# A down-projection in seven products of half operands instead of eight

## The chip, the cores and the metric

The kernel runs on one core of one Trainium2 chip. The metric is the device time of one execution in microseconds, lower is better. Matmuls run on TensorE (PE, with its weight loads as PEld), elementwise work on VectorE (DVE) and ScalarE (ACT), small work and some transfers on GpSimd (POOL), and most transfers are issued by SyncE (SP).

## What is computed

One block of a streaming encoder over 512 tokens of width 1024: a state-space mixer and a latent attention side by side, a cross-attention to 256 memory tokens, and a feed-forward part with a causal convolution, each added to the residual x. The feed-forward part and the end are what matters here:

```python
u = causal_depthwise_conv(h @ w_up, conv_w, conv_b)      # h: 512 x 1024, w_up: 1024 x 5632
g, val = jnp.split(u, 2, axis=-1)
x = x + (jax.nn.silu(g) * val) @ w_down                  # 512 x 2816 times 2816 x 1024
return rmsnorm(x, norm_final_w)
```

## The kernel before, in words

All operands are float32. Before a matmul each is split into a high and a low part of the type that TensorE takes (`split`, L92: a cast on ScalarE, then a subtraction on VectorE), and `mm3` (L101 to L105) makes three matmuls of each product: high by high, high by low, low by high. So one k-tile of 128 for one token tile of 128 is three matmuls of 512 columns.

Weights come in pages. `wload` (L145) has SP load 512 KB into one of three raw buffers (`wr`), `wsplit` (L150) splits it into one of four pairs (`wh`, `wl`), and `wpage` (L162) does both.

The up-projection runs over 11 pairs j of feature tiles (L1139). A pass makes two tiles of the gate half and two of the value half: 24 matmuls each into one of three accumulator banks, a convolution of three taps (`conv`, L1125: one ScalarE and two VectorE operations), the gate (`gate`, L1133), and in `evac` (L1151) the product of the two, 128 features by 512 tokens, which is split into high and low there and then (`acts`, L1112 to L1117, 22 tiles). `h3t` (L1054) holds the split input of the up-projection in the tiles tagged Ah and Al, `cbuf` the convolution's buffers.

The down-projection is `down` (L1163): the tokens are four tiles of 128, the output is two halves of 512 columns (`nh`), k runs over 22 tiles, two to a page. `down(0, ...)` makes the left half for all four token tiles, so its 11 pages serve 24 matmuls each; `down(1, (0, 1))` and `down(1, (2, 3))` make the right half for two token tiles at a time and load and split the 11 pages again. In the last call the last token tile is worked in two halves of 256 columns, and the last three pages are held back and run bank by bank, so that the sums of one bank run beside the matmuls of the next. Each finished bank is added to x in SBUF (L1193) and squared and summed (`sq_part`, L196). `finish` (L1198) adds the sums, raises them to -0.5 on POOL, scales one half on VectorE and one on ScalarE by that factor and the norm's weights (`frow`), and stores them from SP's and ScalarE's queues.

The order of instructions on each engine and queue is set when the program is built: a scheduler places them by program order among those that are ready in its own timing. The banks of PSUM are acc (3), tr (2), s (2) and pv (1). Buffers with one tag are handed on when the last reader of the earlier tile is done.

Of the kernel before, what the change touches and what calls it, by code (L numbers as in the profile page):

```python
# [62 lines left out]
def tile_block(ctx, tc, x, mem, positions, norm_mix_w, w_in, ssd_conv_w, ssd_conv_b, ssd_dt_bias,  # L63
# [37 lines left out]
    def mm3(acc, lhs, rhs, first, last):  # L101
        (lh, ll), (rh, rl) = lhs, rhs
        nc.tensor.matmul(acc, lhsT=lh, rhs=rh, start=first, stop=False)  # L103
        nc.tensor.matmul(acc, lhsT=lh, rhs=rl, start=False, stop=False)  # L104
        nc.tensor.matmul(acc, lhsT=ll, rhs=rh, start=False, stop=last)  # L105
# [1006 lines left out]
    acts = []  # L1112
    for tag in ("Bh", "Bl"):
        tl = base.tile([P, 4, 2, T], F32R, name="actB", tag=tag, bufs=1)
        acts += [tl[:, i] for i in range(4)]
    acts += [page("act") for _ in range(5)]
    acts += [k4([P, 2, T], "act", F32R) for _ in range(9)]  # L1117
# [21 lines left out]
    for j in range(FM // 2):  # L1139
# [8 lines left out]
        for m in range(2):  # L1148
            mi = 2 * j + m

            def evac(a):  # L1151
                th = ths[m]
                nc.vector.tensor_tensor(th, th, conv(a, FM + mi, "uv"), ALU.mult)
                split(acts[mi][:, 0], acts[mi][:, 1], th)
            gemm_fm(pv_, m, h3t, T, evac)

# [4 lines left out]
    nc.vector.memset(ssf, EPS)  # L1161

    def down(nh, ts_, staggered=False):  # L1163
        full, halves = (slice(0, 512),), (slice(0, 256), slice(256, 512))
        cols = {t: halves if staggered and t == ts_[-1] else full for t in ts_}
        accs = {}
        for t in ts_:
            for c in cols[t]:
                accs[t, c.start] = (acc_bank() if len(accs) < 3 else s_bank())[:, 0:c.stop - c.start]
        held = []  # L1170

        def add(t, kp, page, c):
            hi, lo = page
            for k in range(2):
                kt = 2 * kp + k
                mm3(accs[t, c.start], (acts[kt][:, 0, tsl(t)], acts[kt][:, 1, tsl(t)]), (hi[:, k, c], lo[:, k, c]),
                    kt == 0, kt == FM - 1)

        for kp in range(FM // 2):
            v = w_ffn_down[0][kp * 2 * P:(kp + 1) * 2 * P, nh * 512:(nh + 1) * 512].rearrange("(k p) c -> p k c", p=P)  # L1180
            page = wpage(v, 2, 512)
            if staggered and kp >= FM // 2 - 3:
                held.append((kp, page))
            else:
                for t in ts_:
                    for c in cols[t]:
                        add(t, kp, page, c)
        for t in ts_:
            for i, c in enumerate(cols[t]):
                for kp, page in held:  # L1190
                    add(t, kp, page, c)
                xs_ = xt[t][:, nh * 512 + c.start:nh * 512 + c.stop]
                nc.vector.tensor_tensor(xs_, accs[t, c.start], xs_, ALU.add)  # L1193
                sq_part(xs_, ssf[:, t, 1 + nh + i:2 + nh + i], fin[:, 2, c], float(D) ** -0.5)
            if nh:
                finish(t, 2 + len(cols[t]))

    def finish(t, n):  # L1198
        rs = small([P, 1], "rs")
        nc.gpsimd.tensor_tensor(rs, ss_total(ssf[:, t, 0:n]), neg_half, ALU.pow)  # L1200
        a, b = xt[t][:, 0:512], xt[t][:, 512:]
        nc.vector.scalar_tensor_tensor(b, b, rs, frow[:, 512:], ALU.mult, ALU.mult)
        nc.sync.dma_start(out[0, tsl(t), 512:], b)
        nc.scalar.activation(a, a, AF.Copy, scale=rs)
        nc.scalar.dma_start(out[0, tsl(t), 0:512], a)

    down(0, range(NT))
    for t in range(NT):
        nc.vector.tensor_tensor(xt[t][:, 0:512], xt[t][:, 0:512], frow[:, 0:512], ALU.mult)
# [27 lines left out]
```

## Time and profile before

| what | us |
|---|---|
| median of 3 runs (lowest, highest) | 984.88 (982.55, 985.73) |
| the profiled execution, its own time | 982.37 |
| its span, first to last instruction | 980.6 |
| TensorE busy, granted clock | 966.8, 0.999 |
| VectorE busy | 667.3 |
| ScalarE busy | 522.2 |
| POOL busy | 187.3 |

The span is what the trace covers; the profiled execution's own time has 1.8 us around it. Busy times are shares of the span and stages differ, so the stretch of the down-projection, from about 853 us on, is read by itself below. A matmul's busy time overlaps that of the next; what one costs is the distance of their starts.

### The profile page before, as it was taken

Reading aid. Unit: us, or ns where it says so; the run is one execution under the profiler, and the core shown is the slowest. Engines: PE = TensorE matmul, PEld = TensorE weight load, DVE = VectorE, ACT = ScalarE, POOL = GpSimd, SP = SyncE. Lnnn points to the kernel's source line nnn. Section 1 sums busy time; section 2 is a strip of 40 time slices with the busy share of each in tenths; the row PEclk is TensorE's granted clock in tenths of the full one; section 3 lists DMA queues with packets and bytes.
Section 4 is the critical chain, followed back from the end, with each engine's and each line's share of the span. In section 5 each row is a group of like instructions: output and inputs, shape, how many; then the busy total and the mean of one; then the engine's idle time right before and its main releaser. Section 6 shows DMA issues by size and latency. Waiting matters only on the chain.

```text
span 980.6 us, 14908 instructions
## 1 busy us (share of the span) xinstructions
PE 966.8 (99%) x5405; PEld 844.0 (86%) x5405; DVE 667.3 (68%) x1208; ACT 522.2 (53%) x1076; POOL 187.3 (19%) x298
## 2 busy tenths in 40 slices
PE   9999999999999999999999999999999999999997
PEld 8889898999998999988878888888888888888886
DVE  5989999969888778854745436776666666622553
ACT  5678776666677777753534334534444444421442
POOL 2016546346352442110101100000000000000000
PEclk9999999999999999999999999999999999999999
DMA  7653432325532445232332120433233223333462
GB/s 233 198 181 99 129 97 80 108 63 189 168 97 74 134 158 187 85 131 86 109 106 66 65 86 25 131 115 96 87 101 108 93 86 103 111 109 102 148 223 86
DMA packets 90305, 114.06 MB, mean 116 GB/s; under 512 B 5799, under 2 KB 70119, under 8 KB 89848
## 3 DMA queue, kind: packets, MB, share of 16 engines
q1 hardware_dynamic: 87960, 105.73, 34.0%
q0 software_dynamic: 1696, 6.33, 2.1%
q8 instruction: 43, 0.70, 0.3%
q10 hardware_dynamic: 576, 1.05, 0.3%
q14 instruction: 30, 0.25, 0.1%
HBM read 104.67 MB, written 8.42 MB: 115 GB/s over the span
## 4 chain that ended last, share of the span: by engine, by line
PE 82%; DVE 5%; ACT 4%; POOL 3%; DMA 3%; issue 2%; POOLq 0%; ACTq 0%; DVEq 0%
PE acc L104 22%; PE acc L103 22%; PE acc L105 22%; PE tr L119 3%; PE s L103 3%; DMA aE<-acT 3%; PE s L104 3%; PE s L105 3%; PE pv L821 2%; DVE wl L95 1%; ACT aE L554 1%; PE acc L119 1%; POOL rsy L142 1%; ACT wh L94 1%; DVE xn L1070 1%
## 5 line engine op out<-in xcount | busy, mean ns | idle before, releaser
L95 DVE TENSOR_TENSOR wl<-wr,wh 128x1024 fp32r<-128x1024 f32 (+3 forms) x161 | 196.1, 1222 | 134.7 <-ACT wh L94 134.0
L94 ACT CAST wh<-wr 128x1024 fp32r<-128x1024 f32 (+3 forms) x161 | 165.0, 1030 | 173.8 <-PE acc L104 72.2
L103 PE MATMUL acc<-Ah,wh 128*128 128x512 f32 (+1 forms) x560 | 216.1, 386 | 2.0 <-ACT Ah L94 1.5
L104 PE MATMUL acc<-Al,wh 128*128 128x512 f32 (+1 forms) x560 | 215.6, 385 | 0.1
L105 PE MATMUL acc<-Ah,wl 128*128 128x512 f32 (+1 forms) x560 | 215.1, 384 | 0.0
L103 PEld LDWEIGHTS acc<-Ah,wh 128*128 128x128 f32 x560 | 105.2, 188 | 22.4 <-ACT Ah L94 2.0
L104 PEld LDWEIGHTS acc<-Al,wh 128*128 128x128 f32 x560 | 105.3, 188 | 20.4 <-DVE Al L95 0.8
L105 PEld LDWEIGHTS acc<-Ah,wl 128*128 128x128 f32 x560 | 105.3, 188 | 19.7
L1129 DVE SCALAR_TENSOR_TENSOR cbuf<-acc,fcw,cbuf 128x511 f32<-128x511 f32 (+1 forms) x88 | 65.6, 747 | 26.6 <-ACT cbuf L1127 25.1
L103 PE MATMUL acc<-wh,Ah 128*128 128x256 f32 (+2 forms) x240 | 76.8, 322 | 0.1
L104 PE MATMUL acc<-wl,Ah 128*128 128x256 f32 (+2 forms) x240 | 76.3, 318 | 0.0
L105 PE MATMUL acc<-wh,Al 128*128 128x256 f32 (+2 forms) x240 | 76.0, 318 | 0.0
L1200 POOL TENSOR_TENSOR rs<-ss,neg_half 128x1 f32<-128x1 f32 x4 | 2.2, 549 | 358.5 <-DVE ss L201 358.5
L805 POOL TENSOR_SCALAR p<-p,ri 128x128 f32<-128x128 f32 (+1 forms) x64 | 36.1, 567 | 109.9 <-DVE ri L804 101.5
L103 PEld LDWEIGHTS acc<-wh,Ah 128*128 128x128 f32 x240 | 46.0, 192 | 3.1 <-DVE x L959 0.5
L104 PEld LDWEIGHTS acc<-wl,Ah 128*128 128x128 f32 x240 | 46.1, 192 | 2.4
L105 PEld LDWEIGHTS acc<-wh,Al 128*128 128x128 f32 x240 | 46.1, 192 | 2.4 <-DVE Al L95 0.2
L1127 ACT ACTIVATE cbuf<-acc,fcb,fcw 128x512 f32<-128x512 f32 x44 | 34.3, 779 | 23.9 <-PE acc L105 23.9
L104 PE MATMUL acc<-wl,act 128*128 128x512 f32 (+1 forms) x112 | 40.5, 363 | 0.0
L103 PE MATMUL acc<-wh,act 128*128 128x512 f32 (+1 forms) x112 | 40.5, 363 | 0.0
L105 PE MATMUL acc<-wh,act 128*128 128x512 f32 (+1 forms) x112 | 40.4, 363 | 0.0
L103 PE MATMUL acc<-wh,Bh 128*128 128x256 f32 x128 | 37.1, 290 | 0.0
(377 smaller groups left out, 2241.1 us busy)
## 6 DMA issues: line engine op xcount, KB each, us to landing
wr<-in_w_ffn_up_dram SPq DMA_DIRECT2D x44, 512.0 KB, 3.5
wr<-in_w_ffn_down_dram SPq DMA_DIRECT2D x33, 512.0 KB, 3.3
wr<-in_w_in_dram SPq DMA_DIRECT2D x26, 512.0 KB, 3.8
wr<-in_w_out_dram SPq DMA_DIRECT2D x16, 512.0 KB, 3.9
aE<-acT POOLq DMA_DIRECT2D x16, 256.0 KB, 3.7
wr<-in_w_mem_k_dram SPq DMA_DIRECT2D x8, 512.0 KB, 4.3
wr<-in_w_mem_v_dram SPq DMA_DIRECT2D x8, 512.0 KB, 3.3
wr<-in_w_mem_q_dram SPq DMA_DIRECT2D x8, 512.0 KB, 4.3
```

The source lines that it names most:

```text
L94: first = nc.scalar.copy(hi, src)
L95: nc.vector.tensor_tensor(lo, src, f32(hi), ALU.subtract)
L103: nc.tensor.matmul(acc, lhsT=lh, rhs=rh, start=first, stop=False)
L104: nc.tensor.matmul(acc, lhsT=lh, rhs=rl, start=False, stop=False)
L105: nc.tensor.matmul(acc, lhsT=ll, rhs=rh, start=False, stop=last)
L119: nc.tensor.transpose(dst, src, ident[:n, :n])
L142: nc.gpsimd.tensor_tensor(rs, ms, neg_half, ALU.pow)
L554: nc.scalar.activation(E[:, h], E[:, h], AF.Relu, scale=-1.0, bias=cenT[:, c, hh:hh + 1])
L805: nc.gpsimd.tensor_scalar(p_, p_, ri, 1.0, ALU.mult, ALU.mult)
L821: nc.tensor.matmul(acc[:, kt * P:], lhsT=lhs, rhs=PT[:, i, 4 * kt:3 * kt + NT], start=(kt == 0 and i == 0), stop=(kt == NT - 1 and i == 1))
L1127: nc.scalar.activation(u, acc, AF.Identity, scale=fcw[:, 2, m:m + 1], bias=fcb[:, m:m + 1])
L1129: nc.vector.scalar_tensor_tensor(u[:, s:], acc[:, :T - s], fcw[:, 2 - s, m:m + 1], u[:, s:], ALU.mult, ALU.add)
```

## The change

The tokens are taken in two halves, k in two interleaved halves (tile i = 0 and i = 1 of each pair) and the output in two halves. That makes each operand four quarters, and the down-projection eight products of quarters (256 tokens by 1408 by 512). The change makes seven products instead, of quarters and of sums of quarters, by a scheme of Strassen's kind.

On the side of the activations, `evac` stores the raw product, and after every second j `prepare` splits the two quarters that the first two products need (`slot`) and forms the first sums with three VectorE operations. A later quarter or sum is split (`then=`) a product ahead, group by group of two k-tiles.

On the side of the weights, the sums are made by transfers: `more` has POOL issue a transfer that adds a quarter of w_down to one that lies in SBUF (`tw`, the kept quarter, and `yw`), after that page has been split for the running product. Order: P2 (b21), P1 (tw), P5 (tw), P6 (tw), P3 (yw), P7 (yw) and the last, P4 (tw). Additions follow P1, P5, P6 and P3. A product has six pages, five of two k-tiles and one of one. P6, P3 and P7 go on in the banks of earlier products, which are read in between. The space for POOL's descriptors is set to 8192 in the last line; `kept8` and `spare` are new tiles.

```diff
--- before.py
+++ after.py
@@ -98,11 +98,11 @@
             nc.scalar.activation(hi, src, AF.Copy, scale=scale)
             nc.vector.scalar_tensor_tensor(lo, src, scale, f32(hi), ALU.mult, ALU.subtract)
 
-    def mm3(acc, lhs, rhs, first, last):
+    def mm3(acc, lhs, rhs, first, last, more=False):
         (lh, ll), (rh, rl) = lhs, rhs
-        nc.tensor.matmul(acc, lhsT=lh, rhs=rh, start=first, stop=False)
-        nc.tensor.matmul(acc, lhsT=lh, rhs=rl, start=False, stop=False)
-        nc.tensor.matmul(acc, lhsT=ll, rhs=rh, start=False, stop=last)
+        nc.tensor.matmul(acc, lhsT=lh, rhs=rh, start=first, stop=False, skip_group_check=more)
+        nc.tensor.matmul(acc, lhsT=lh, rhs=rl, start=False, stop=False, skip_group_check=more)
+        nc.tensor.matmul(acc, lhsT=ll, rhs=rh, start=False, stop=last, skip_group_check=more)
 
     def tsl(t):
         return slice(t * P, (t + 1) * P)
@@ -1109,12 +1109,49 @@
                 scaled(3)
                 turn(3)
                 store(3)
-    acts = []
+
+    NG = (FM // 2 + 1) // 2
+    HT = T // 2
+    gsz = [min(2, FM // 2 - 2 * g) for g in range(NG)]
+    rawu = []
     for tag in ("Bh", "Bl"):
-        tl = base.tile([P, 4, 2, T], F32R, name="actB", tag=tag, bufs=1)
-        acts += [tl[:, i] for i in range(4)]
-    acts += [page("act") for _ in range(5)]
-    acts += [k4([P, 2, T], "act", F32R) for _ in range(9)]
+        tl = base.tile([P, 4, 2, T], F32, name="rawB", tag=tag, bufs=1)
+        rawu += [tl[:, i] for i in range(4)]
+    slotu = [page("slot") for _ in range(5)]
+    for n in range(9):
+        if n % 3 == 2:
+            rawu.append(k4([P, 2, T], "raw"))
+        else:
+            slotu.append(k4([P, 2, T], "slot", F32R))
+
+    def raw_of(g, i):
+        return rawu[2 * g + i] if g < NG - 1 else rawu[2 * g][:, i:i + 1]
+
+    def quarter(g, i, half):
+        return raw_of(g, i)[:, :, HT * half:HT * (half + 1)]
+
+    def slot(g, s):
+        n = gsz[g]
+        u = slotu[2 * g + s].rearrange("p i (n t) -> p i n t", n=2) if n == 2 else \
+            slotu[2 * g].rearrange("p i (n t) -> p i n t", n=2)[:, s].unsqueeze(2)
+        return u[:, 0], u[:, 1]
+
+    sums = {}
+    spare = [base.tile([P, 2, HT], F32, name="spare")]
+
+    def prepare(g):
+        a11, a21, a12, a22 = (quarter(g, i, h) for i in range(2) for h in range(2))
+        split(*slot(g, 1), a12)
+        split(*slot(g, 0), a11)
+        s1 = spare.pop()[:, 0:gsz[g]]
+        nc.vector.tensor_tensor(s1, a21, a22, ALU.subtract)
+        nc.vector.tensor_tensor(a21, s1, a11, ALU.subtract)
+        nc.vector.tensor_tensor(a12, a12, a21, ALU.add)
+        sums[g] = {"s1": s1, "s2": a21, "s4": a12, "a22": a22}
+        spare.append(a11)
+
     cbuf = kx([P, 6, T], "cbuf")
     rot_ = {}
 
@@ -1150,65 +1187,154 @@
 
             def evac(a):
                 th = ths[m]
-                nc.vector.tensor_tensor(th, th, conv(a, FM + mi, "uv"), ALU.mult)
-                split(acts[mi][:, 0], acts[mi][:, 1], th)
+                nc.vector.tensor_tensor(raw_of(j // 2, m)[:, j % 2], th, conv(a, FM + mi, "uv"), ALU.mult)
             gemm_fm(pv_, m, h3t, T, evac)
+        if j % 2 or j == FM // 2 - 1:
+            prepare(j // 2)
 
 
     fin = kx([P, 3, T], "fin")
     frow = row_tile(fin[:, 0:2].rearrange("p a n -> p (a n)"), norm_final_w)
     ssf = small([P, NT, 4], "ssf", 1)
     nc.vector.memset(ssf, EPS)
-
-    def down(nh, ts_, staggered=False):
...
+    c0, c1 = slice(0, 512), slice(512, D)
+    wdv = w_ffn_down[0].rearrange("(k i p) c -> i p k c", i=2, p=P)
+
+    def wq(g, i, n):
+        return wdv[i][:, 2 * g:2 * g + gsz[g], 512 * n:512 * (n + 1)]
+
+    def fetch(dst, g, i, n):
+        nc.sync.dma_start(dst, wq(g, i, n))
+        return dst
+
+    def more(dst, g, i, n):
+        nc.gpsimd.dma_start(dst, wq(g, i, n), accum_op=ALU.add)
+
+    kept = []
+    for tag in ("Ah", "Al"):
+        tl = base.tile([P, 4, 2, 512], F32, name="kept", tag=tag, bufs=1)
+        kept += [tl[:, i] for i in range(4)]
+    kept.append(base.tile([P, 2, 512], F32, name="kept8"))
+    b21 = [wload(wq(g, 1, 0), gsz[g], 512) for g in range(3)]
+    tw = []
+    for g in range(NG):
+        tw.append(fetch(kept[g][:, 0:gsz[g]], g, 0, 0))
+        if g >= 3:
+            b21.append(wload(wq(g, 1, 0), gsz[g], 512))
+
+    def product(banks, s, raws, first=True, then=None):
+        for g in range(NG):
+            hi, lo = wsplit(raws[g])
+            ah, al = slot(g, s)
+            for t in range(2):
+                for k in range(gsz[g]):
+                    mm3(banks[t], (ah[:, k, tsl(t)], al[:, k, tsl(t)]), (hi[:, k], lo[:, k]),
+                        first and g == k == 0, g == NG - 1 and k == gsz[g] - 1, not first)
+            if then:
+                then(g)
+
+    def add(banks, t0, c, op=ALU.add):
+        for t in range(2):
+            xs_ = xt[t0 + t][:, c]
+            if op == ALU.add:
+                nc.vector.tensor_tensor(xs_, banks[t], xs_, ALU.add)
             else:
-                for t in ts_:
-                    for c in cols[t]:
-                        add(t, kp, page, c)
-        for t in ts_:
-            for i, c in enumerate(cols[t]):
-                for kp, page in held:
-                    add(t, kp, page, c)
-                xs_ = xt[t][:, nh * 512 + c.start:nh * 512 + c.stop]
-                nc.vector.tensor_tensor(xs_, accs[t, c.start], xs_, ALU.add)
-                sq_part(xs_, ssf[:, t, 1 + nh + i:2 + nh + i], fin[:, 2, c], float(D) ** -0.5)
-            if nh:
-                finish(t, 2 + len(cols[t]))
-
-    def finish(t, n):
+                nc.vector.tensor_tensor(xs_, xs_, banks[t], ALU.subtract)
+
+    def square(t, c, i):
+        sq_part(xt[t][:, c], ssf[:, t, i:i + 1], fin[:, 2, 0:c.stop - c.start], float(D) ** -0.5)
+
+    def ready(t0, c):
+        for t in (t0, t0 + 1):
+            square(t, c, 1)
+            nc.vector.tensor_tensor(xt[t][:, c], xt[t][:, c], frow[:, c], ALU.mult)
+
+    def finish(t, n, early, late):
         rs = small([P, 1], "rs")
         nc.gpsimd.tensor_tensor(rs, ss_total(ssf[:, t, 0:n]), neg_half, ALU.pow)
-        a, b = xt[t][:, 0:512], xt[t][:, 512:]
-        nc.vector.scalar_tensor_tensor(b, b, rs, frow[:, 512:], ALU.mult, ALU.mult)
-        nc.sync.dma_start(out[0, tsl(t), 512:], b)
+        a, b = xt[t][:, early], xt[t][:, late]
+        nc.vector.scalar_tensor_tensor(b, b, rs, frow[:, late], ALU.mult, ALU.mult)
+        nc.sync.dma_start(out[0, tsl(t), late], b)
         nc.scalar.activation(a, a, AF.Copy, scale=rs)
-        nc.scalar.dma_start(out[0, tsl(t), 0:512], a)
-
-    down(0, range(NT))
-    for t in range(NT):
-        nc.vector.tensor_tensor(xt[t][:, 0:512], xt[t][:, 0:512], frow[:, 0:512], ALU.mult)
-    down(1, (0, 1))
-    down(1, (2, 3), staggered=True)
+        nc.scalar.dma_start(out[0, tsl(t), early], a)
+
+    rb = [s_bank() for _ in range(2)]
+    product(rb, 1, b21)
+    add(rb, 0, c0)
+    ub = [tr_bank() for _ in range(2)]
+    yw = [kept[NG + i][:, 0:gsz[i]] for i in range(3)] + [None] * 3
+
+    def after_p1(g):
+        more(tw[g], g, 0, 1)
+        split(*slot(g, 1), sums[g]["s1"])
+        if g < 3:
+            fetch(yw[g], g, 1, 1)
+
+    product(ub, 0, tw, then=after_p1)
+    add(ub, 0, c0)
+    ready(0, c0)
+    vb = [acc_bank() for _ in range(2)]
+
+    def after_p5(g):
+        more(tw[g], g, 1, 1)
+        split(*slot(g, 0), sums[g]["s2"])
+        if g >= 3:
+            yw[g] = wload(wq(g, 1, 1), gsz[g], 512)
+
+    product(vb, 1, tw, then=after_p5)
+    add(vb, 2, c1)
+
+    def after_p6(g):
+        more(tw[g], g, 1, 0)
+        split(*slot(g, 1), sums[g]["s4"])
+
+    product(ub, 0, tw, first=False, then=after_p6)
+    add(ub, 0, c1, ALU.subtract)
+
+    def after_p3(g):
+        more(yw[g], g, 0, 1)
+        s3 = sums[g]["s2"]
+        nc.vector.scalar_tensor_tensor(s3, s3, -1.0, sums[g]["a22"], ALU.mult, ALU.subtract)
+        split(*slot(g, 0), s3)
+
+    product(vb, 1, yw, first=False, then=after_p3)
+    add(vb, 0, c1)
+    for t in range(2):
+        square(t, c1, 2)
+        finish(t, 3, c0, c1)
+    product(ub, 0, yw, first=False, then=lambda g: split(*slot(g, 1), sums[g]["a22"]))
+    add(ub, 2, c1, ALU.subtract)
+    ready(2, c1)
+    add(ub, 2, c0)
+
+    halves = (slice(0, 256), slice(256, 512))
+    parts = [(0, s_bank(), c0)] + [(1, (acc_bank() if i else s_bank())[:, 0:256], c) for i, c in enumerate(halves)]
+
+    def last(g, page, which):
+        hi, lo = page
+        ah, al = slot(g, 1)
+        for t, acc, c in which:
+            for k in range(gsz[g]):
+                mm3(acc, (ah[:, k, tsl(t)], al[:, k, tsl(t)]), (hi[:, k, c], lo[:, k, c]),
+                    g == k == 0, g == NG - 1 and k == gsz[g] - 1)
+
+    held = []
+    for g in range(NG):
+        page_ = wsplit(tw[g])
+        if g < NG - 3:
+            last(g, page_, parts)
+        else:
+            held.append((g, page_))
+    for i, part_ in enumerate(parts):
+        for g, page_ in held:
+            last(g, page_, [part_])
+        t, acc, c = part_
+        xs_ = xt[2 + t][:, c]
+        nc.vector.tensor_tensor(xs_, acc, xs_, ALU.add)
+        square(2 + t, c, 2 + (i == 2))
+        if i != 1:
+            finish(2 + t, 3 + (i == 2), c1, c0)
 
 
 _INS = ['x', 'mem', 'positions', 'norm_mix_w', 'w_in', 'ssd_conv_w', 'ssd_conv_b', 'ssd_dt_bias',
@@ -1221,7 +1347,7 @@
     import concourse.bacc as _bacc
     from concourse.bass_utils import run_bass_kernel_spmd as _run
 
-    nc = _bacc.Bacc("TRN2", target_bir_lowering=False, num_devices=1)
+    nc = _bacc.Bacc("TRN2", target_bir_lowering=False, num_devices=1, dynamic_dma_scratch_size=8192)
     arrays, args = {}, []
     named = [(n, np.ascontiguousarray(inputs[n])) for n in _INS]
     named[-1] = ('norm_final_w', named[-1][1].reshape(1, D))
```

## Rows read from the trace of the kernel before

**Rows 1.** The page: span, busy time by engine, and the chain that ended last.

```profile
span 980.6 us, 14908 instructions
PE 966.8 (99%) x5405; PEld 844.0 (86%) x5405; DVE 667.3 (68%) x1208; ACT 522.2 (53%) x1076; POOL 187.3 (19%) x298
...
PE 82%; DVE 5%; ACT 4%; POOL 3%; DMA 3%; issue 2%; POOLq 0%; ACTq 0%; DVEq 0%
```

**Rows 2.** Windows of the up-projection and the down-projection (columns in the first line).

```profile
core 0: us, PE busy (x) PEld busy (x) DVE busy (x) ACT busy (x) POOL busy (x), PEclk, DMA share, GB/s
...
700.00:720.00 20.00, 20.00 (x90) 16.57 (x89) 13.43 (x18) 8.03 (x11) 0.00 (x0) 1.00 0.34 106
...
860.00:880.00 20.00, 20.00 (x90) 16.57 (x89) 4.90 (x4) 4.22 (x4) 0.00 (x0) 1.00 0.37 127
880.00:900.00 20.00, 20.00 (x90) 16.57 (x89) 4.90 (x4) 4.22 (x4) 0.00 (x0) 1.00 0.27 84
...
940.00:960.00 20.00, 20.00 (x124) 17.98 (x123) 11.41 (x13) 10.10 (x14) 1.07 (x2) 1.00 0.73 238
```

**Rows 3.** Timeline: first load, first matmuls of passes, last matmul, POOL's wait, end.

```profile
841.84 13.97 SPq L147 DMA_DIRECT2D wr<-in_w_ffn_down_dram  x4
...
853.13 0.39 PE L103 MATMUL acc<-wh,actB 128*128 128x512 f32 x1
...
942.89 0.39 PE L103 MATMUL acc<-wh,actB 128*128 128x512 f32 x1
...
945.61 1.07 POOL L1200 TENSOR_TENSOR rs<-ss,neg_half 128x1 f32<-128x1 f32 x2 [330.37 <-DVE ss L201]
...
973.70 0.28 PE L105 MATMUL acc<-wh,act 128*128 128x256 f32 x1
...
976.65 0.35 ACTq L1205 DMA_DIRECT2D out_dram<-x  x1
```

**Rows 4.** Groups of instructions from 853 us on, by shape: busy us, mean ns, idle before.

```profile
L95 DVE TENSOR_TENSOR wl<-wr,wh 128x1024 fp32r<-128x1024 f32 x30 | 36.8, 1225 | 63.0 <-ACT wh L94 62.7
...
L94 ACT CAST wh<-wr 128x1024 fp32r<-128x1024 f32 x30 | 31.6, 1053 | 67.5 <-PE s L105 35.1 <-PE acc L105 29.4 <-DMA wr<-in_w_ffn_down_dram 1.9
...
L1193 DVE TENSOR_TENSOR x<-acc,x 128x512 f32<-128x512 f32 x6 | 3.9, 684 | 5.2 <-PE acc L105 5.2
...
L1202 DVE SCALAR_TENSOR_TENSOR x<-x,rs,fin 128x512 f32<-128x512 f32 x4 | 2.9, 750 | 1.9 <-POOL rs L1200 1.9
...
L95 DVE TENSOR_TENSOR act<-cbuf,act 128x512 fp32r<-128x512 f32 x2 | 1.4, 688 | 0.7 <-ACT act L94 0.7
L1193 DVE TENSOR_TENSOR x<-acc,x 128x256 f32<-128x256 f32 x2 | 0.8, 424 | 1.1 <-PE acc L105 1.1
...
L94 ACT CAST act<-cbuf 128x512 fp32r<-128x512 f32 x1 | 0.6, 621 | 2.8 <-DVE cbuf L1153 2.8
```

**Rows 5.** One line's loads after 840 us (ns to issue, us to landing); stores.

```profile
L147 SPq DMA_DIRECT2D wr<-in_w_ffn_down_dram x30: 367/368/390, 841.8 to 956.8; - x30
...
DMA to landing us min/median/max: 3.2/3.4/4.4
...
out_dram<-x ACTq DMA_DIRECT2D x4, 256.0 KB, 3.9
out_dram<-x SPq DMA_DIRECT2D x4, 256.0 KB, 4.1
```

**Rows 6.** POOL's own transfers (ns to issue), and the window in which they lie.

```profile
L547 POOL DMA_DIRECT2D aE<-acT x16: 538/603/768, 57.1 to 195.3; - x16
...
57.00:203.00 146.00, 145.00 (x953) 132.03 (x952) 130.51 (x237) 108.96 (x247) 75.29 (x95) 1.00 0.35 102
```

**Rows 7.** Windows of fullest transfers: rows of 8 KB (365 us), of 2 KB (938, 948).

```profile
365.00:366.00 1.00, 1.00 (x8) 0.96 (x7) 0.17 (x1) 0.72 (x3) 0.88 (x3) 1.00 1.08 412
...
938.00:940.00 2.00, 2.00 (x11) 1.65 (x10) 1.23 (x1) 0.70 (x1) 0.00 (x0) 1.00 0.81 249
...
948.00:950.00 2.00, 2.00 (x19) 2.00 (x18) 0.32 (x1) 1.05 (x1) 0.00 (x0) 1.00 0.96 347
```

More of the change, by code (lines that the diff above doesn't have):

```diff
@@ L1161, in tile_block @@
     nc.vector.memset(ssf, EPS)
-    def down(nh, ts_, staggered=False):
-        full, halves = (slice(0, 512),), (slice(0, 256), slice(256, 512))
-        cols = {t: halves if staggered and t == ts_[-1] else full for t in ts_}
-        accs = {}
-        for t in ts_:
-            for c in cols[t]:
[L1169 to L1183, printed above, removed]
-            else:
-                for t in ts_:
-                    for c in cols[t]:
-                        add(t, kp, page, c)
-        for t in ts_:
-            for i, c in enumerate(cols[t]):
-                for kp, page in held:
-                    add(t, kp, page, c)
-                xs_ = xt[t][:, nh * 512 + c.start:nh * 512 + c.stop]
-                nc.vector.tensor_tensor(xs_, accs[t, c.start], xs_, ALU.add)
-                sq_part(xs_, ssf[:, t, 1 + nh + i:2 + nh + i], fin[:, 2, c], float(D) ** -0.5)
-            if nh:
-                finish(t, 2 + len(cols[t]))
```

## The prediction

> **What bounds the kernel now.** I read the page first: TensorE is busy 99% of the span and heads the chain of waits with 82% [rows 1]. Then the windows by stage: from 700 us to the end of the products TensorE is busy all of each stretch at a granted clock of 1.00 (the 2.4 GHz level), while VectorE stands at 13.4 of 20 us in the up-projection and 4.9 to 11.4 of 20 in the down-projection, and the transfers at 0.27 to 0.73 [rows 2]. So a removed matmul is removed time, as long as its replacement work fits beside what is left. Then the timeline, for the price of a matmul: the first two passes of the down-projection run from 853.13 to 942.89 us, 396 matmuls of 512 columns (264 for the left half of the output, 132 for tokens 0 and 1 of the right half): 89.76/396 = 0.2267 us each [rows 3]. The busy time of one (0.39 us) overlaps the next and is no price. The last pass, 66 whole and 132 of 256 columns, ends about 0.12 us after 973.70: 30.93 us, which leaves (30.93 - 14.96)/132 = 0.121 us for a half one. The down-projection is thus 120.7 us of matmuls, and 6.8 us of sums, scaling and storing follow [rows 3].
>
> **Products.** The change makes seven products of 11 x 2 x 3 = 66 matmuls, the last with half its columns cut in two: 429 x 0.2267 + 66 x 0.121 = 105.2 us. Gain **15.5 us**. One product lasts L = 14.96 us; a page of two k-tiles 12 x 0.2267 = 2.72 us, the last, half page 1.36 us. The products keep banks apart (P2 s, P1, P6 and P7 tr, P5 and P3 acc), and each bank is read one product before it is written again, so no matmul waits for a sum.
>
> **Splits and sums.** From [rows 4]: a page split is 1.05 us on ScalarE and 1.23 on VectorE; a 512-element operation 0.62 and 0.69, a 256-element one 0.42 on either. Per product the weights take 5 x 1.23 + 0.69 = 6.8 us of VectorE and the next activation quarter 5 x 0.69 + 0.42 = 3.9 us. Additions of a bank into x are 2 x 0.68 = 1.4 us. P3 also forms the third activation sum, 3.9 us: 6.8 + 3.9 + 3.9 + 1.4 = 16.0 us, 1.0 over L. P5 has 13.4 (two scalings of x for 1.4), P7 13.9 (1.8 us to finish tokens 0 and 1), P1 and P6 12.1, P4 about 11. P1 to P7 sum to 67.5 us of 74.8, 90%. ScalarE has 5.9 + 3.5 and a few squares, 11 at most. An activation quarter is split a whole product before its use, so the 1.0 us of P3 can lag into P7; I cost the lag, and VectorE waiting for ScalarE's cast page by page, at 1 us, the excess of P3 (0 if the lag hides, 8 us if every product paid 1.6).
> In the up-projection two passes lose two of four splits and gain three operations: ScalarE -1.2 us, VectorE +0.7 us per 43.5 us. It has a third of its time free there [rows 2], and nothing in that loop made TensorE wait; cost 0, and at most 6 x 0.7 = 4 us if that cover were gone.
>
> **Plain loads.** SP issues 18 loads (six quarters' pages each of the first three weight blocks, three of them half size) for 33; the 0.37 us issues fall, cost 0. The first pages are early as now: the first down-projection load is issued at 841.84, before its use at 853.13 [rows 3, 5]. The new tiles for the kept quarter lie where the up-projection's input lay, so they start at about 853; if SP sets four of them ahead of the fourth page of P2, that page lands about 5 x 1.5 + 1.9 = 9.4 us after 853 and must land 3 x 2.72 - 2.3 = 5.9 us after: 3.5 us lost. The program can issue it as soon as the page three before is split (before 853), so I take 0.5 us, near the lower end of 0 to 3.5.
>
> **Adding transfers.** This decides. After P1, P5, P6 (into tw) and P3 (into yw) each split page gets another quarter added in its place: 4 x 5.5 = 22 units of 512 KB. POOL issues them; it is idle 330 us there [rows 3], and an issue of its queue takes 0.60 us [rows 6], 24 of them 14.4 us, hidden. Each waits on POOL for VectorE's split; behind them stand only the two small powers for tokens 0 and 1, due later. Who waits for the landing is ScalarE's cast in the next product, and with it all behind it on ScalarE.
> No row shows an adding transfer. Lower bound: a plain load of the same rows. The fullest 2 us stretch with such rows moved 347 GB/s at share 0.96, so 0.524 MB take 1.51 us [rows 7]. Upper bound: no overlap at all, a load's landing of 3.4 us and a store's 4.0 us in a row, 7.4 us [rows 5]. I take two reads (the weight and the old sum) at the load's rate, a = **3.0 us**: writes are a part of the plain load's 1.51 us already, so the extra is the second read.
> The Trainium skill, Collectives: The Full Stack, "The bandwidth ceiling: the fold count and why AG ≠ RS ≠ AR", says an adding transfer runs at half the rate of a copy because it reads two sources, and gives 31 GB/s for an engine; my estimate from it is 2.1 us for a unit, and the sum would lose nothing at all. No run here shows it yet.
> How much fits: four split buffers let the first page of P1 be split 6.8 us (2.72 + 2.72 + 1.36) before P1's first matmul; after 1.05 + 1.23 us its addition starts, at -4.5 us. The last page of P7 is due at 4 L + 5 x 2.72 = 73.4 us, less 1.3 for its split and 1.9 (3.4 - 1.5) for landing. In these 74.7 us the 16 engines carry 22 a and about 5 us of the plain yw pages (8.3 us in all, the rest before): a may be (74.7 - 5)/22 = **3.17 us**. At 3.0 it fits with 3 us over; each microsecond of a beyond costs 22 us. So 0 is taken.
> A rule against the change: the Trainium skill, SBUF — State Buffer, "Who interferes with whom", warns that a VectorE operation in its two-port mode keeps POOL from writing descriptors. The rows speak for little of it: POOL's 16 issues took 0.54 to 0.77 us in a stretch where VectorE was busy 130.5 of 146 us [rows 6]. By the rule at its worst, a wait of one page split per issue, POOL would need 24 x (0.6 + 1.2) = 43 us of 75 and still lose nothing.
>
> **Sum.** -15.5 + 1.0 + 0.5 = -14.0 us. The end (bank into x, square, power, scaling, store) keeps its operations and its 6.8 us. The profiled execution took 982.37 us, 1.8 more than its span of 980.6, and comes to 968.4; the median of the runs is 984.88, 2.5 us higher, so I give **971 us**.
>
> **Rivals.**
> 1. The queue of additions binds (slower). Place: casts of P6 and P7 waiting for landings. It decides from a = 3.17 on and takes back all 14 us at a = 3.17 + 14/22 = 3.81. If an addition costs three passes (two reads and a write apart) a = 4.53: 22 x 1.36 = 29.9 us lost, **1001 us**; without overlap 22 x 4.2 = 93 us, 1064. For it: no row has such a transfer, and other down-projection stretches moved 249 GB/s at share 0.81 [rows 7], 3.4 us by two reads. Against it: long rows reached 412 GB/s [rows 7].
> 2. The additions take between 3.2 and 3.95 us, at the edge: 974 to 988, around no change.
> 3. VectorE binds: 90% by the sum, in order, behind ScalarE at every page. Against: it was busy 130.5 of 146 us earlier while TensorE stood still 1 us [rows 6]. At 1.6 us a product, 5 products: 7 us more than taken, **978 us**.
> 4. SP's order in P2: 3.5 us instead of 0.5, **974 us**.
>
> **Chances.** Forecast 0.52, rival 3 0.12, rival 4 0.05, rival 2 0.08 (0.03 of it faster, 0.04 level, 0.01 slower), rival 1 0.21, and 0.02 for a level result of causes not seen. Runs of the kernel before differ by 0.3% (982.55 to 985.73), so less than 3 us cannot be told from no change. Faster 0.72, same 0.06, slower 0.22. The forecast's own range is 966 (nothing lost) to 975; to hold 8 in 10 the range goes on through rivals 2 to 4 to rival 1 at three passes: 966 to 1001.
>
> **What would show it.** Right: 462 whole-matmul equivalents 0.227 us apart with TensorE full from about 853 to 959; adding transfers queued one behind the other, landing in about 5 us, some 3 us of transfer time each; VectorE near 13 of 15 us. Wrong: ScalarE's cast of the weights waiting for a transfer and TensorE for that cast, most of all in P7; then the spacing of landings gives a. If instead the cast is early and VectorE's split late, it is rival 3; a gap only in the first 10 us of the down-projection is rival 4.

## The result and the profile after

The changed kernel takes 969.4 us (median of 4 runs, 968.1 to 970.0), the kernel before 983.7 (4 runs, 982.3 to 985.7): a ratio of **0.985** [0.983, 0.988], 14.3 us less. The forecast was 971. The profiled execution of after took 970.01 us over a span of 968.1, the one of before 982.37 over 980.6: 12.5 us less between the two traces that are compared here.

The page of after, its span, busy times, the queue of the adding transfers and the chain, beside [rows 1]:

```profile
span 968.1 us, 14844 instructions
...
PE 953.8 (99%) x5306; PEld 832.4 (86%) x5306; DVE 701.5 (72%) x1269; ACT 536.2 (55%) x1105; POOL 215.0 (22%) x322
...
q0 software_dynamic: 7712, 17.86, 8.7%
...
PE 86%; DVE 4%; ACT 4%; DMA 3%; POOL 2%; issue 1%; SPq 0%; POOLq 0%; ACTq 0%
```

TensorE issues 99 matmuls fewer and is busy 13.0 us less. VectorE gains 34 us, ScalarE 14, POOL 28, and the chain of waits leads through TensorE more than before (86 against 82%). Before, queue q0 moved 6.33 MB; the 11.5 MB more are the four sets of 2.88 MB that the adding transfers bring.

The timeline of after at the places of [rows 3]: the six pages of the first product, its first matmul, the first kept page, POOL's first addition, the last matmul, the last store:

```profile
825.62 30.26 SPq L147 DMA_DIRECT2D wr<-in_w_ffn_down_dram  x6
...
855.95 0.39 PE L103 MATMUL s<-wh,slot 128*128 128x512 f32 x1
...
856.14 2.00 SPq L1207 DMA_DIRECT2D kept<-in_w_ffn_down_dram  x4
...
867.22 1.28 POOL L1211 DMA_DIRECT2D kept<-in_w_ffn_down_dram  x1 [249.17 <-DVE wl L95]
...
961.06 0.28 PE L105 MATMUL acc<-wh,slot 128*128 128x256 f32 x1
...
964.01 0.37 ACTq L1259 DMA_DIRECT2D out_dram<-x  x1
```

The seven products begin at 855.95 and end about 0.12 us after 961.06: 105.23 us where eight took 120.7. The end behind them is as long as before (last matmul's start to the end of the span: 7.0 us, before 6.9). But the down-projection begins 2.8 us later than before (853.13). So the traces read: -15.5 in the products, +2.8 ahead of them, +0.1 at the end, -12.5 in all; the 2.8 us are taken apart below.

Windows of after, in the up-projection, in the stretches of [rows 2], while the additions run (874 to 930, and four microseconds of it), and after them:

```profile
core 0: us, PE busy (x) PEld busy (x) DVE busy (x) ACT busy (x) POOL busy (x), PEclk, DMA share, GB/s
700.00:720.00 20.00, 20.00 (x90) 16.57 (x89) 15.60 (x20) 8.65 (x11) 0.00 (x0) 1.00 0.34 105
...
862.00:864.00 2.00, 2.00 (x11) 1.65 (x10) 2.00 (x6) 0.50 (x1) 0.00 (x0) 1.00 1.04 397
...
874.00:930.00 56.00, 56.00 (x249) 46.37 (x248) 46.03 (x59) 33.40 (x50) 24.77 (x22) 1.00 1.12 202
...
878.00:882.00 4.00, 4.00 (x19) 3.31 (x18) 3.14 (x5) 1.81 (x3) 0.88 (x1) 1.00 1.13 207
...
916.00:931.00 15.00, 15.00 (x68) 12.41 (x67) 11.43 (x15) 8.73 (x13) 4.68 (x5) 1.00 1.06 185
...
932.00:934.00 2.00, 2.00 (x11) 1.65 (x10) 2.00 (x3) 1.87 (x6) 0.00 (x0) 1.00 0.03 6
...
940.00:960.00 20.00, 20.00 (x116) 17.60 (x116) 11.38 (x15) 6.95 (x12) 0.25 (x1) 1.00 0.01 2
```

TensorE is full in each, at a granted clock of 1.00; from 850 us on the view of waits has no row for TensorE at all. The transfers are at their limit from 874 to 930 us (share 1.12; with more of them, in e2 below, the fullest windows show 205 to 207 GB/s too) and have nothing left to do from 932 on, when the product that uses the last sum (P7, from 930.8) has run for 1 us. All of it lies beside the matmuls.

The additions, POOL's line 1211 by itself (ns to issue, us to landing), and the rows of the waits from 850 us on that concern them:

```profile
L1211 POOL DMA_DIRECT2D kept<-in_w_ffn_down_dram x21: 884/1203/1310, 867.2 to 918.4; - x21
L1211 POOL DMA_DIRECT2D wr<-in_w_ffn_down_dram x3: 899/1203/1203, 920.3 to 923.5; - x3
...
DMA to landing us min/median/max: 7.1/8.6/10.8
```

```profile
POOL kept L1211 <- DVE wl L95: 274.7, 19, 249.2
...
ACT slot L94 <- PE tr L104: 12.5, 10, 1.6
...
DVE wl L95 <- ACT wh L94: 7.4, 13, 1.8
```

POOL waits for VectorE's split, as it should. ScalarE waits for a matmul that still reads the activation slot, VectorE for ScalarE's cast; no engine waits for an addition to land.

### The profile page after: what moved, and what is told of

The parts are those of the page before. It is cut to its first block, busy times and chain, and to the rows that moved or that the text cites. A ratio compares the mean times of both kernels' runs of the same rounds, so it can differ in the third digit from the quotient of the medians.

```text
span 968.1 us, 14844 instructions
## 1 busy us (share of the span) xinstructions
PE 953.8 (99%) x5306; PEld 832.4 (86%) x5306; DVE 701.5 (72%) x1269; ACT 536.2 (55%) x1105; POOL 215.0 (22%) x322
## 3 DMA queue, kind: packets, MB, share of 16 engines
q0 software_dynamic: 7712, 17.86, 8.7%
## 4 chain that ended last, share of the span: by engine, by line
PE 86%; DVE 4%; ACT 4%; DMA 3%; POOL 2%; issue 1%; SPq 0%; POOLq 0%; ACTq 0%
PE acc L103 21%; PE acc L104 21%; PE acc L105 21%; PE tr L119 4%; PE s L103 3%; PE s L104 3%; PE s L105 3%; DMA aE<-acT 2%; PE pv L821 2%; PE tr L104 2%; PE tr L105 2%; PE tr L103 2%; ACT aE L554 1%; PE acc L119 1%; DVE wl L95 1%
## 5 line engine op out<-in xcount | busy, mean ns | idle before, releaser
L95 DVE TENSOR_TENSOR wl<-wr,wh 128x1024 fp32r<-128x1024 f32 (+3 forms) x140 | 168.2, 1205 | 74.6 <-ACT wh L94 73.9
L94 ACT CAST wh<-wr 128x1024 fp32r<-128x1024 f32 (+3 forms) x140 | 141.5, 1016 | 112.7 <-PE acc L104 77.1
L1211 POOL DMA_DIRECT2D kept<-in_w_ffn_down_dram x21 | 24.5, 1182 | 277.1 <-DVE wl L95 274.7
L95 DVE TENSOR_TENSOR wl<-kept,wh 128x1024 fp32r<-128x1024 f32 (+1 forms) x30 | 34.4, 1148 | 5.4 <-ACT wh L94 5.4
L95 DVE TENSOR_TENSOR PT<-tr,PT 128x128 fp32r<-128x128 f32 (+1 forms) x64 | 30.5, 480 | 9.2 <-PE pv L821 5.5
L94 ACT CAST PT<-tr 128x128 fp32r<-128x128 f32 (+1 forms) x64 | 26.9, 428 | 16.8 <-PE tr L119 15.3
```

Of the source, the lines that this page charges most:

```text
L94: first = nc.scalar.copy(hi, src)
L95: nc.vector.tensor_tensor(lo, src, f32(hi), ALU.subtract)
L1211: nc.gpsimd.dma_start(dst, wq(g, i, n), accum_op=ALU.add)
```

## Experiments

Theory A, which the traces suggest: the gain is the removed matmuls alone, and the additions cost nothing because they fit between the use of a page and its next use. Rivals: the additions already cost something (rival 1 of the prediction, in part); VectorE is the next bound (rival 3); the missing 2.8 us come from the down-projection's own start, or from elsewhere. Each group of runs below has the kernel before on the same chip beside it, and ratios are against that.

### e1: the same transfers without the addition

```diff
-        nc.gpsimd.dma_start(dst, wq(g, i, n), accum_op=ALU.add)
+        nc.gpsimd.dma_start(dst, wq(g, i, n))
```

The sums of the weights are left out; each quarter overwrites the one before.

> POOL's 24 transfers load their quarter over the old one instead of adding to it (the sums of the weights are left out, so the output is of other weights). Queue theory (additions cost 2.56 us of the 16 engines each for 512 KB, all hidden with some 12 us to spare): the time stays at the changed kernel's, 969 us within 1.5; from 874 to 930 us the transfers' share falls from 1.12 to about 0.6, a landing from 8.6 to 4 to 5 us, a unit near 1.5 us. Rival (the additions already hold some products back): 2 to 6 us faster.

Measured: 969.9 us, ratio 0.986 [0.983, 0.990], the time of after. Its window of 52 us with the transfers, and POOL's line:

```profile
874.00:926.00 52.00, 52.00 (x231) 43.09 (x230) 42.83 (x56) 31.34 (x46) 13.79 (x20) 1.00 0.59 200
```

```profile
L1211 POOL DMA_DIRECT2D kept<-in_w_ffn_down_dram x21: 567/722/802, 865.3 to 916.4; - x21
...
DMA to landing us min/median/max: 3.6/4.4/7.7
```

The same 200 GB/s occupy the 16 engines to 0.59 instead of 1.12: an addition takes 1.9 times the engine time of a plain transfer, and 1.20 us of POOL instead of 0.72. Halving that load changes nothing in the time that these runs can tell, and in the traces nothing at all: the first and the last matmul of the down-projection in e1,

```profile
853.99 0.39 PE L103 MATMUL s<-wh,slot 128*128 128x512 f32 x1
...
959.10 0.28 PE L105 MATMUL acc<-wh,slot 128*128 128x256 f32 x1
```

lie 105.11 us apart, in after 961.06 - 855.95 = 105.11. The additions are hidden whole.

The edit changes one thing more. POOL's queue moves the same 17.86 MB as in after, but in 4896 packets instead of 7712, 128 fewer for each of the 22 units. The additions go in packets of 2 KB, the plain transfers of e1 in packets of 4 KB. The page of e1, and in after the addition of a half page:

```profile
q0 software_dynamic: 4896, 17.86, 5.6%
```

```profile
878.57 0.88 POOL L1211 DMA_DIRECT2D kept<-in_w_ffn_down_dram  x1 [0.65 <-DVE wl L95]
```

The half page of an addition and the whole page of e1 have 128 data packets each, and their issues take 0.88 and 0.72 us. So the longer issue may belong to the number of packets as much as to the addition.

### e2: 12 additions more

```diff
     def after_p1(g):
         more(tw[g], g, 0, 1)
+        if g >= 3:
+            more(tw[g - 3], g - 3, 0, 1)
```

and the like in `after_p5`, `after_p6` and `after_p3`: 34 units of 512 KB instead of 22. Three pages of each set have a quarter added twice, so the sums of the weights are others.

> After each of the four products with additions, the first three pages get their addition a second time, three pages later: 34 units of 512 KB instead of 22 (the output is of other sums). Queue theory: 34 x 2.56 = 87 us no longer fit into the some 75 us between the first split of P1 and the last page of P7, and the repeated page is due early in the next product; worked out page by page the loss is 27 to 32 us, a time of 995 to 1002 us, with ScalarE's cast of the kept weights waiting for transfers. Rival (the engines have reserve, a unit is really about 1.5 us and the share above 1 is only waiting): 0 to 2 us, 969 to 972.

Measured: 1006.2 us, ratio 1.023 [1.020, 1.025], 36.8 us more than after and 22 more than before, and more than the 995 to 1002 us that the queue theory gave. The waits from 850 us on, of ScalarE, TensorE and POOL:

```profile
ACT wh L94 <- DMA kept<-in_w_ffn_down_dram: 50.7, 9, 13.6
...
POOL kept L1211 <- DMA kept<-in_w_ffn_down_dram: 36.2, 8, 12.2
...
PE tr L103 <- ACT wh L94: 18.0, 4, 8.3
...
PE acc L103 <- ACT wh L94: 3.5, 1, 3.5
```

Here is the picture that the prediction gave for its rival 1: the cast waits for a transfer, TensorE for the cast. A rise of 36.8 us is more than TensorE's waits add up to (18.0 + 3.5 + 0.9 + 0.5 = 22.9). Windows of e2 show the rest:

```profile
914.00:918.00 4.00, 0.00 (x0) 0.00 (x0) 0.01 (x1) 1.08 (x2) 1.39 (x2) 0.69 1.13 207
918.00:922.00 4.00, 3.95 (x9) 2.65 (x9) 3.35 (x5) 0.80 (x3) 1.20 (x1) 0.50 1.13 205
...
958.00:962.00 4.00, 3.96 (x10) 3.02 (x10) 0.76 (x2) 0.07 (x1) 2.14 (x2) 0.50 1.13 207
```

From 914 to 918 TensorE stands still and the granted clock begins to fall; from 918 to 922 it is busy, but at 0.50, the 1.2 GHz level, and has 9 matmuls where after has 19 in four microseconds (878 to 882). Between the first and the last matmul of the down-projection e2's trace is at 0.50 for 27.3 us, after's never. In 8 of these TensorE stands still anyway; 19.4 us at half the clock are 9.7 us lost, an estimate from these two numbers. With the waits of 22.9 that is 32.6 of the 36.0 us between the two spans; the other 3 are not taken apart. So a queue of transfers that is too long is paid for twice, in the wait and in the clock after it.

Not all of the waiting is for the engines of the transfers. One of TensorE's four long waits lasts 8.3 us, up to 957 us; a window within it, and POOL's issues there:

```profile
950.00:952.00 2.00, 0.00 (x0) 0.00 (x0) 0.00 (x0) 0.00 (x0) 1.64 (x2) 1.00 0.31 56
```

```profile
950.36 3.74 POOL L1211 DMA_DIRECT2D kept<-in_w_ffn_down_dram  x3 [12.19 <-DMA kept<-in_w_ffn_down_dram]
```

POOL had waited 12.19 us for an addition to land before it issued the next to the same page, and behind it the queue ran nearly empty, 56 GB/s, while TensorE stood still. The repeated additions thus cost by their order too, and e2 doesn't give the price of a longer queue by itself.

### e4: more work for VectorE

```diff
             hi, lo = wsplit(raws[g])
+            nc.vector.tensor_tensor(lo[:, 0], raws[g][:, 0], f32(hi[:, 0]), ALU.subtract)
```

One k-tile of each page has its subtraction made twice in the first six products: 36 x 0.69 = 24.8 us of VectorE.

> In the six products before the last, VectorE makes the low part of each page's first 512 columns a second time with the same result: 36 x 0.69 = 24.8 us more work in the some 90 us of these products, where it was busy 72. Theory (VectorE has that reserve, no product waits for it now): it comes to about 97 of 90 us and binds, 5 to 12 us slower, 974 to 981. Rival (VectorE is already the limit by its order and its waits for ScalarE): the full 24.8 us, 994. Rival (it has far more reserve than its busy time says): under 2 us.

Measured: 975.3 us, ratio 0.991 [0.988, 0.994], 5.9 us more than after, as the theory had it. The products without the last one's end, in one window, and two rows of the waits:

```profile
855.00:945.00 90.00, 86.09 (x369) 69.84 (x368) 85.79 (x125) 50.48 (x75) 30.47 (x26) 0.98 0.93 196
...
874.00:878.00 4.00, 4.00 (x13) 3.10 (x12) 4.00 (x6) 1.49 (x2) 1.78 (x2) 0.58 0.59 100
```

```profile
PE tr L104 <- DVE wl L1228: 2.1, 1, 2.1
...
PE acc L104 <- DVE wl L1228: 1.7, 2, 0.9
```

With VectorE busy 85.8 of 90 us TensorE stands for 3.9 us of them, and again pays in the clock (0.58 in 874 to 878). In after VectorE has about a fifth of its time free here (82% busy from 874 to 930), some 16 to 18 of 90 us; most of the 24.8 fits there, and what doesn't is paid. VectorE is the next bound, but not this kernel's.

### e3: the page that came too early

A timeline of SP at the very start shows what the change put there: the load of `kept8` (L1207), the tile that shares its memory with no earlier one, stands among the first loads of the kernel, some 900 us before its use. The first rows are SP's and the first 512-column product of the input projection's in after, the fence after that the same product in e3:

```profile
11.49 0.43 SPq L1207 DMA_DIRECT2D kept<-in_w_ffn_down_dram  x1
...
30.31 0.50 PE L103 MATMUL acc<-Ah,wh 128*128 128x512 f32 x1
```

```profile
29.65 0.50 PE L103 MATMUL acc<-Ah,wh 128*128 128x512 f32 x1
```

```diff
+    issued = []
     def fetch(dst, g, i, n):
-        nc.sync.dma_start(dst, wq(g, i, n))
+        issued.append(nc.sync.dma_start(dst, wq(g, i, n)).ins)
         return dst
...
         if g < 3:
-            fetch(yw[g], g, 1, 1)
+            with tc.issue_after(issued[0]):
+                fetch(yw[g], g, 1, 1)
```

> Only the load of the page in the new, never shared tile is held on SP until the first kept page of the down-projection has been issued; before, it stood 11.5 us after the start among the first loads. Theory (the 512 KB at the start push the loads of the first stage back and cost 1.2 us there): first product against Ah at 29.4 us as in the kernel before, not 30.6; 1.2 us faster, about 968.2 where the changed kernel has 969.4. Rival (the start is bound otherwise): no change, within 0.5 us.

Measured: 969.2 us, ratio 0.985 [0.982, 0.987]: in the time 0.2 us where 1.2 were expected, no difference that this measurement can tell. In the traces the difference at the start is plain. The start of that product in all profiled executions of this study:

| kernels | us |
|---|---|
| with the early page (after, e1, e2, e4, e6, e7) | 30.05 to 30.50, mean 30.30 |
| without it (e3, e5, e8, e9) | 28.76 to 29.65, mean 29.10 |
| before | 29.05 |

The page in the queue delays the first weights, and the start with them, by about 1.2 us.

Not all of it arrives at the down-projection. Its first matmul, less 1.7 us where the clock was at half for 3.4 us before it and less 0.7 us for ten added matmuls (both below), starts at 853.99 to 855.64 us in the six with the early page (mean 854.5), at 853.34 to 854.54 in the four without it (mean 853.9), and at 853.13 in before. So some 0.7 us are left of the 1.2, with as much scatter within each group, and one execution without the page (e9) is later than four with it.

### e7, e5, e8, e9: the clock after a standstill

The rest of the 2.8 us lies between 490 and 500 us. There TensorE stands for 1.3 us before the first query projection of the cross-attention, in both kernels; and in the profiled execution of after the clock is low behind it. The window in after, one matmul in it, and the same window in e7, which is the changed kernel once more:

```profile
495.00:500.00 5.00, 4.87 (x13) 3.67 (x14) 1.48 (x3) 0.00 (x0) 0.00 (x0) 0.66 0.57 177
```

```profile
494.18 0.49 PE L103 MATMUL acc<-Ah,wh 128*128 128x512 f32 x1 [1.30 <-ACT Ah L94]
...
497.18 0.63 PE L103 MATMUL acc<-Ah,wh 128*128 128x512 f32 x1
```

```profile
495.00:500.00 5.00, 4.88 (x20) 3.86 (x21) 1.47 (x3) 0.00 (x0) 0.00 (x0) 1.00 0.53 170
```

While the clock is down a matmul's busy time is 0.63 us instead of 0.39, and there are 13 in these 5 us where e7 has 20; 7 x 0.227 = 1.6 us are lost.

> The changed kernel itself once more, beside the others of this call: 969.4 within 1.5 us, 0.984 to 0.987 of the kernel before. It is there so that the late page and the ten matmuls are compared with it on one chip.

Measured in e7: 969.7 us (5 runs, 967.3 to 971.1), ratio 0.985 [0.984, 0.987]; the product behind the gap starts at 494.16 in its profiled execution (clock 0.999) and at 494.18 in after's, 492.94 in before's, so up to here both are 1.2 us late, as at the start; the down-projection begins at 854.25 in e7, 855.95 in after, 853.13 before. That takes the 2.8 us of these traces apart: 1.7 for the clock behind the gap, 1.1 from before the gap, and nothing for the up-projection (from the product behind the gap to the down-projection 360.09 us in e7, 360.19 in before). Of the 1.1 the early page explains some 0.7 by the means of e3; the rest is no more than the scatter of these starts, and no run gives it a cause. The clock's part is not made by the change: the mean clock differs as much among the runs of either kernel. Runs of before took 981.6 to 981.7 us at a mean clock of 0.999 and 986.3 at 0.995; runs of after's program 967.3 at 0.998 and 971.1 at 0.994. Where before's slower ones lost it no trace shows.

e5 and e9 (one kernel, run twice) and e8 try to keep TensorE busy in the standstill, beside the edit of e3, with 10 matmuls (5 in e8) whose results nobody uses:

```diff
+    warm = pv_bank()[:, 0:P]
+    for _ in range(10):
+        nc.tensor.matmul(warm, lhsT=ident, rhs=xn2[:, 0, D - P:D], start=True, stop=True)
```

> The kernel with the late page, and ten matmuls of 128 columns whose result nobody reads put on TensorE between the last transposes of the cross-attention's norm and the first query projection, where it stands still for 1.3 us at about 493 us and some executions then show a granted clock of 0.66 in the following 5 us. Theory (the dip follows the standstill): clock 1.00 from 495 to 500 us in every profile, mean clock 0.998 or more, and the median 1 to 2 us under the changed kernel's of the same call; no gain over its best executions. Rival (the dip has nothing to do with the standstill): median as the late page's, mean clock 0.996 to 0.998 as before, or slower by up to 0.5 us for the ten matmuls.

> The late page and five matmuls nobody reads in place of ten (1.2 us of TensorE, as each shows as two of 0.12 us). Theory (the standstill of 1.3 us is what the dip follows, and ten were 0.8 us too many): clock 1.00 from 495 to 500 us, the first product after the gap starts no later than without them, median 967 to 968.5 where ten gave 968.1. Rival (five leave too long a standstill): the dip is back in some executions and the median is that of the late page, 969.2.

> The same with ten, once more beside it: 968.1 within 1 us, no dip from 495 to 500 us. If the earlier 968.12 was chance, 969 to 970.

Measured: e5 968.1 us (967.9 to 969.8), 0.984 [0.983, 0.985]; e8 968.5 (967.1 to 969.3), 0.984 [0.981, 0.986]; e9 968.1 (967.2 to 969.5), 0.983 [0.981, 0.986]. In the three profiled executions the clock is 1.00 from 495 to 500 us. From the last transposes to the product behind the gap it is 2.34 us in after and in e8, 3.02 in e5 and e9: five matmuls lie in the gap at no cost, ten cost 0.7 us. But of the eight executions without them four kept 1.00 behind the gap too (before, e1, e4, e7) and four fell (after, e2, e3, e6), so three without a fall can be chance; and e5 lost its clock elsewhere (0.91 from 240 to 260 us). The medians are 1.0 to 1.6 us under those of the changed kernel (969.4, 969.7); the later page alone, which e5, e8 and e9 share, gave 0.2 in e3, and the ranges overlap. That the matmuls help is not shown; these three are the best that was run, by about 1 us, for a reason that is left open.

### e6: half the space for POOL's descriptors

```diff
-    nc = _bacc.Bacc("TRN2", target_bir_lowering=False, num_devices=1, dynamic_dma_scratch_size=8192)
+    nc = _bacc.Bacc("TRN2", target_bir_lowering=False, num_devices=1, dynamic_dma_scratch_size=4096)
```

> Only the space for POOL's descriptors is halved again, 8192 to 4096. Theory (the 16 engines' rate holds the additions back, not the space in which they are listed): no change, 969 within 1.5 us, additions still 205 GB/s from 878 to 930 us. Rival (the space limits how many additions are under way, so the change's own halving costs something): landings shorter than 8.6 us, issues on POOL longer than 1.2 us, additions ending later than 930 us, and if it goes on to TensorE several us slower.

Measured: 969.7 us, ratio 0.985 [0.984, 0.987]; 203 GB/s at a share of 1.12 from 874 to 930 us, issues of 1.20 us, landings of 6.4 to 11.1: as in after. A space half as large costs nothing, so nothing speaks for a cost of the 8192 that the change sets; a larger one wasn't tried.

## Why the prediction was right

**Products: right.** 105.2 us forecast, 105.23 measured. The distance of two starts [rows 3] was the price of a matmul, with TensorE full on both sides of the change; that it was full is what the other terms had to secure.

**Adding transfers: hidden as forecast, their price too high.** I had 3.0 us for a unit, from two reads at 347 GB/s. At 207 GB/s (878 to 882 us) 0.524 MB take 2.53 us. The step that was off is the plain rate, not the two reads: plain pages of the same rows move at 397 GB/s in after (862 to 864 us), 1.32 us each, and 2.53/1.32 = 1.9. The stretches of [rows 7] with such rows were not at the transfers' limit, and the one of 347 GB/s (948 to 950 us) wasn't loads alone, since stores of the output, which take some 4 us to land [rows 5], were issued just ahead of it:

```profile
946.95 0.97 ACTq L1205 DMA_DIRECT2D out_dram<-x  x2
```

The rule of the Trainium skill, Collectives: The Full Stack, "The bandwidth ceiling: the fold count and why AG ≠ RS ≠ AR", that an adding transfer runs at half the rate of a copy, agrees with these traces (1.9 by the rates, 1.12/0.59 = 1.9 by e1); the 2.1 us that I estimated from its figure for an engine are less than the 2.53 measured. By the prediction's own formula 2.53 us leave 74.7 - 5 - 22 x 2.53 = 14 us to spare instead of 3; the transfers are quiet at 932 us, 11 to 12 us before the last sum is due (P7's sixth page is used from 930.75 + 5 x 2.72 = 944.35 us on, its split takes 1.3: 943). e2 lies beyond the edge, as the formula has it: 34 units need 86 us, 16 more than there are, and TensorE waits for 23. That it is more than 16 is in part POOL's order, which the formula leaves out: it waits 36.2 us for additions to land before it issues the next to the same page, and the queue runs nearly empty behind one of these waits. How much of the 23 us that is was not tried by itself.

**POOL's issue: 1.20 us, not 0.60,** which was a row of another transfer without an addition [rows 6]; e1 has 0.72 in the same place. 24 of them take 29 us of 75, still hidden. The longer issue goes with the addition and with its twice as many packets, which e1 does not separate. That VectorE keeps POOL from writing descriptors, the rule of the Trainium skill, SBUF — State Buffer, "Who interferes with whom", no run here shows: VectorE is busy to 82% in both stretches and the issue differs by the kind of transfer. Nor does the prediction's worst case follow from that section of the Trainium skill, which says that `tensor_tensor`, the operation of the page split, has no two-port mode. The landing took 8.6 us, not some 5: with the engines saturated each waits behind the others.

**VectorE's lag (+1.0): did not come.** The step that failed is P3's 16.0 us. I counted the operations in the product where the program has them; the scheduler placed the third activation sum right behind the split of the quarter that it overwrites, in P1 and P5. The rows of line 1297 in after:

```profile
L1297 DVE SCALAR_TENSOR_TENSOR rawB<-rawB x4: 683/688/691, 876.3 to 883.1; 128x512 f32<-128x512 f32 x4
L1297 DVE SCALAR_TENSOR_TENSOR raw<-raw x2: 411/545/679, 886.3 to 892.0; 128x512 f32<-128x512 f32 x1, 128x256 f32<-128x256 f32 x1
```

P3's window (916 to 931) then has 11.43 of 15 us. The fullest product is P1, and the five from P1 to P7 hold 59.9 us of VectorE's time where I had summed 67.5, so the sum was too high as a whole:

```profile
870.90:885.90 15.00, 15.00 (x68) 12.42 (x67) 13.77 (x19) 8.73 (x13) 6.54 (x7) 1.00 1.11 227
870.90:945.70 74.80, 74.80 (x331) 61.94 (x330) 59.92 (x78) 44.95 (x66) 27.19 (x25) 1.00 0.93 179
```

e4 shows where the limit is.

**SP's order (+0.5): did not come.** The pages of the first product were issued from 825.62 to 855.9, the kept ones from 856.14 on: rival 4 has no place.

**The up-projection at nothing: right.** A stretch of 20 us cuts the loop at other places in the two kernels (13.4 us of VectorE in [rows 2], 15.6 in after); over two whole passes, 43.5 us, before and then after, VectorE gains 0.4 us (forecast 0.7) and ScalarE loses 1.2 (as forecast):

```profile
656.60:700.10 43.50, 43.50 (x193) 36.04 (x192) 29.35 (x37) 18.87 (x24) 0.00 (x0) 1.00 0.32 97
```

```profile
658.60:702.10 43.50, 43.50 (x194) 36.02 (x193) 29.74 (x38) 17.71 (x22) 0.00 (x0) 1.00 0.32 97
```

TensorE stayed full from 640 us on, and e7 has no time lost between the gap at 494 us and the down-projection.

**What I did not see** is the load that slid to the start of the kernel, 1.2 us there and some 0.7 at the down-projection. I had looked at where the new tiles' memory came free and not at the one whose memory was never taken. Without the clock's part, which runs of both kernels have, the traces give -15.5 + 1.1 + 0.1 = -14.3 us, the difference of the medians; I had -15.5 + 1.0 + 0.5 = -14.0. The total is right for the products; the two small terms were wrong ones, and others that I had not named took their place. That the sum came within 0.3 us is luck to that extent. **Rival 1** is refuted for 22 units by e1 and confirmed as a mechanism by e2, beside POOL's order; **rival 2** goes with it (2.53 is under 3.17); **rival 3** needs the 24.8 us of e4.

## What to carry to other kernels

A product fewer of Strassen's kind is worth its matmuls at their spacing if the sums are made by an engine or queue with room, and if each sum is there before its next use: count units times the price of one against that time, and take the price as twice that of a plain transfer at the full rate of the same rows (1.9 here). Past that edge the cost is steep, since the long waits of TensorE in e2 and e4, 2.1 to 8.3 us, each brought a stretch at half the clock. A new tile that shares its memory with nothing lets the scheduler load it at once, where it may stand in front of what the kernel waits for; tying its load to a later one moved the start by 1.2 us here, though no gain in the time was shown for it by itself.

## What was unexpected of the hardware

- After a standstill of 1.3 us the granted clock fell in some executions (0.66 over the next 5 us in after, e2, e3 and e6) and not in others (1.00 in before, e1, e4 and e7, with the same standstill). Runs of one kernel differ by 0.3 to 0.4%, and the slower ones have the lower mean clock (0.994 or 0.995 against 0.998 or 0.999).
- After longer waits TensorE ran at 0.50 though busy again (e2, 918 to 922 and 958 to 962 us).
- A queue of adding transfers saturates at 202 to 207 GB/s, at an engine share of 1.12 to 1.13, so the share is not a scale that ends at 1.
- POOL's adding transfers went in twice as many packets as its plain ones of the same bytes (7712 against 4896 packets in its queue as a whole, in after and e1).
